# Seven-product down projection of a decoder trunk: other product signs, DMA-accumulated weight sums, a new buffer layout and a new last chunk

## Chip, cores and metric

The kernel runs on one NeuronCore of a Trainium2 chip. The metric is the device time of one execution in microseconds. Profiled times are counted from the start of the profiled span, which is a little shorter than the execution's own time.

## The reference, cut to what matters

One decoder layer over 512 tokens of width 2048 (float32): a token mixer of four head groups, a cross-attention, and an MLP with a squared ReLU, then a final RMS norm. The change lies in the MLP and the norm after it; the rest of the layer is untouched.

```python
hn = rmsnorm(h, norm_mlp_g[l])                                   # h: 512 x 2048
u = jnp.square(jax.nn.relu(jnp.einsum('bld,df->blf', hn, w_up[l])))   # 512 x 8192
h = h + jnp.einsum('blf,fd->bld', u, w_down[l])                  # w_down: 8192 x 2048
return rmsnorm(h, norm_final_g)
```

## The kernel before

Every float32 matrix is split into a high part in float32r (a ScalarE copy that rounds) and a low part (VectorE, the value minus the high part). A product is then three TensorE matmuls: high by high, high by low, low by high.

**Up phase.** Eight chunks q of 1024 hidden channels, in four pairs each. `up_pair` runs two `gemm`s of 16 k-tiles over the token activations (`ah{k}`, `al{k}`, 16 tiles each of 2 KB per partition, from the pool "acts"; weights stream through `wr`, `wh`, `wl` of the pool "weights"). It then squares the ReLU on ScalarE into `z`, forms four combinations of token and channel blocks of `z` on VectorE (L976 to L979), splits all seven operands (L146, L147) and lets the POOL queue write them to DRAM (`ud`, L984).

**Down phase.** The 2x2x2 block product (two token halves, two halves of the chunk's channels, two halves of the 2048 output columns) is made with seven products instead of eight. For each chunk, `down_chunk` loads four weight blocks b22, b11, b12, b21, each as two tiles of 1 MB (halves j), and calls `down_product(q, idx, ...)` seven times, idx being 6, 0, 4, 5, 2, 3, 1, in the last chunk 6, 0, 4, 5, 3, 2, 1. A product loads its left operand (`u_load`: two DMAs of 512 KB on SP's queue, three buffers), and for four quarters (j, a) forms the weight combination in place if there is one (L1059, VectorE), rounds it (L1061, ScalarE) and takes the low part (L1062, VectorE) into one of five pairs of tiles `w2h`, `w2l` (`w_tiles`). Then come 48 matmuls into four PSUM banks (`two`, `sm` and `mm`, `acc` in turn), and `evict` adds the banks to accumulators x1 to x7 in SBUF (L1082, VectorE; in chunk 0 a plain ScalarE copy for those that start empty, L1080). The combinations cost 16 VectorE instructions in a chunk: 8 for idx 4 (b12 - b11, then b22 minus that), 4 for idx 5, 4 for idx 2.

Accumulators 2, 3, 4 and 7 start from the residual, which `h_block` transposes and stores to DRAM (`xd`) ahead of the up phase. `merge` (L1102) combines accumulators in the last three chunks. `tail_sums`, `tail_rs`, `tail_out` and `tail` make the final norm: sums of squares on ScalarE, the reciprocal root as a chain of small VectorE instructions, the scaling on VectorE, the store on SP's queue.

**Order and buffers.** A scheduler orders the instructions of each engine, before the kernel is built, by its own model of time; `urgent()` raises priority. At run time each engine and each DMA queue works through its list in order and waits for semaphores. The pools of the down phase lie over memory of the up phase: `down_a` (right side) over the residual tiles, free early in the up phase, and `down` (left side) over weights, activations and the tiles of `up_pair`; a tile waits for those that it covers. `hold` fixes which tiles lie at the bottom of `down`: accumulators 3, 1, 6, 7, then three of the five weight pairs, two of the three u buffers, and four of the eight raw tiles.

Of the kernel before, what the change touches and what calls it, by code (L numbers as in the profile page):

```python
# [20 lines left out]
P = 128  # L21
# [35 lines left out]
def trunk(ctx, tc, A, out):  # L57
# [7 lines left out]
    def pool(name, bufs=1, **kw):  # L65
        return ctx.enter_context(tc.tile_pool(name=name, bufs=bufs, **kw))
# [1 line left out]
    cp = pool("consts")  # L68
    wa = ExitStack()
    wp = wa.enter_context(tc.tile_pool(name="weights", bufs=1))  # L70
    ap = wa.enter_context(tc.tile_pool(name="acts", bufs=1))
    ps = pool("psum", space=PSUM)
    dr = pool("dram", space=DRAM)

# [255 lines left out]
    XL_ = [None] * KT  # L330

    def act_tiles(k):
        h = ap.tile([P, L], F32R, name=f"ah{k}")
        l = ap.tile([P, L], F32R, name=f"al{k}")
        return h, l

    rsx = cp.tile([P, L], F32, name="rsx")
# [402 lines left out]
    def attn_pair(c):  # L740
# [6 lines left out]
        for hd in range(2):  # L747
# [4 lines left out]
        k = ap.tile([P, L], F32, name=f"ah{8 + c % 2}")  # L752
        Q.dma_start(k, qkv_d[4 + c])
        q = []
        for hd in range(2):
            qz = ap.tile([P, L], F32, name=f"a{'hl'[hd]}{10 + c % 2}")
# [234 lines left out]

    zc.close()
    wa.close()
    p2 = pool("down", side="left", reuse_waits="tile")
    acc, first = {}, {}

    def slot(p, name, shape, dt):
        if name in first:
            return first.pop(name)
        return p.tile(shape, dt, name=name)  # L1000

    def hold(name, shape, dt):
        first[name] = p2.tile(shape, dt, name=name)

    ACC, RAW, UT, WT = [P, 2, 2, L], [P, 4, L], [P, 4, 256], [P, 2, L]
    for i in (3, 1, 6, 7):
        hold(f"x{i}", ACC, F32)
    for n in range(2, 5):
        hold(f"w2h{n}", WT, F32R)
        hold(f"w2l{n}", WT, F32R)  # L1010
    for n in range(1, 3):
        hold(f"u{n}0", UT, F32R)
        hold(f"u{n}1", UT, F32R)
    for n in range(4, 8):
        hold(f"wq{n}", RAW, F32)

    def acc_tile(i, eng=G):
        t = slot(p2, f"x{i}", ACC, F32)
        if (i, 0) in xd:
            for b in range(2):  # L1020
                eng.dma_start(t[:, b].rearrange("p j n -> p (j n)"), xd[i, b])
        acc[i] = t

    def flat(t):
        return t.rearrange("p a n -> p (a n)")

    raws, us, ws = [0], [0], [0]

    def raw2():
        n = raws[0] % 8  # L1030
        raws[0] += 1
        return slot(p2a if n < 4 else p2, f"wq{n}", RAW, F32)

    def u_load(q, idx):
        n = us[0] % 3
        us[0] += 1
        uu = []
        for i in range(2):
            t = slot(p2 if n else p2a, f"u{n}{i}", UT, F32R)
            Q.dma_start(t.bitcast(F32), ud[q, i][:, idx])  # L1040
            uu.append(t)
        return uu

    def w_tiles():
        n = ws[0] % 5
        ws[0] += 1
        return [slot(p2 if n > 1 else p2a, f"w2{c}{n}", WT, F32R) for c in "hl"]

    sets = [True]

    def down_product(q, idx, w, comb, acc_to, last=None):
        with urgent():
            uu = u_load(q, idx)
            wt = {}
            for j in range(2):
                for a in range(2):
                    r = [x[j][:, 2 * a:2 * a + 2] for x in (w,) + tuple(t for c in comb for t in c)]
                    for c in range(0, len(r) - 1, 3):
                        V.tensor_tensor(flat(r[c + 1]), flat(r[c + 2]), flat(r[c + 3]), op=OP.subtract)  # L1059
# [37 lines left out]
                    evict(j, b)  # L1097

    def merge(o, a, b, op):
        for h in range(2):  # L1100
            x, y, z = (flat(acc[i][:, h]) for i in (o, a, b))
            V.tensor_tensor(x, y, z, op=op)  # L1102

    def down_chunk(q):
        last = q == NC_ - 1
        with urgent():
            b22, b11, b12, b21 = [], [], [], []
            for b, i, k in ((b22, 1, 1), (b11, 0, 0), (b12, 0, 1), (b21, 1, 0)):
                for j in range(2):
                    t = raw2()  # L1110
                    Q.dma_start(t, A["w_down"][q, i, k, :, j])
                    b.append(t)
        if q == 0:
            acc_tile(3, Q)
            acc_tile(1)
            acc_tile(6)
        down_product(q, 6, b22, (), (-3,) if last else (3,))
        if q == 0:
            for i in (7, 4, 5, 2):
                acc_tile(i)  # L1120
# [4 lines left out]
        down_product(q, 4, b22, ((b12, b12, b11), (b22, b22, b12)), (6,))  # L1125
        down_product(q, 5, b11, ((b11, b22, b11),), (7,))
        if last:
            merge(3, 3, 6, OP.add)
            merge(7, 7, 6, OP.add)
            merge(4, 7, 4, OP.subtract)  # L1130
            down_product(q, 3, b12, (), (3, 7))
            tail_sums(1, 1, 7)
            tail_sums(0, 1, 3)
            down_product(q, 2, b22, ((b22, b22, b21),), (-4,))
            tail_sums(1, 0, 4)
            tail_rs(slice(2, 4))
            down_product(q, 1, b21, (), (2,), tail)
        else:
            down_product(q, 2, b22, ((b22, b22, b21),), (4,))
            down_product(q, 3, b12, (), (5,))  # L1140
            if q == NC_ - 2:
                merge(7, 7, 5, OP.add)
                merge(4, 4, 5, OP.add)
                merge(3, 5, 3, OP.subtract)
            down_product(q, 1, b21, (), (2,))

    ssq = cp.tile([P, 4, 4], F32, name="sx")
    rf = cp.tile([P, 4], F32, name="rf")
# [3 lines left out]

    def tail_sums(t, i, a):
        if not fin:
            fin["g"] = flat(raw2())
            Q.dma_start(fin["g"], A["fin_row"].to_broadcast([P, D]))
            fin["sq"] = flat(raw2())
# [17 lines left out]
    def tail(b):  # L1175
        with urgent():
# [97 lines left out]
```

## Time and profile before

| | us |
|---|---|
| time, median of 3 runs (2136.93 to 2142.98) | 2141.01 |
| the profiled execution's own time | 2139.84 |
| its span | 2138.1 |
| TensorE busy (98% of the span) | 2090.8 |
| VectorE busy (72%) | 1546.4 |
| ScalarE busy (42%) | 905.3 |
| GpSimd busy (4%) | 84.7 |

A busy time is the union of an engine's instruction spans. Matmuls overlap in the pipeline (one takes 0.39 us from start to end, the next starts after some 0.23 us), so the distance from start to start says more than the duration.

### The profile page before, as it was taken

What the parts mean: (1) busy time and instruction counts of PE and PEld (TensorE: products, weight loads), DVE (VectorE), ACT (ScalarE), POOL (GpSimd) and SP (SyncE); (2) the same over time, 40 slices, a digit from 0 to 9 for tenths busy, and PEclk for the clock granted to TensorE, in tenths of its full rate; (3) what the DMA queues carried; (4) which work ended last, traced back from release to release, by engine and by line L of the source; (5) the groups of instructions that cost most, each with busy time, mean ns of one, the idle gap of its engine ahead of it and who ended that gap; (6) DMA issues with size and microseconds to landing.
All of it is one profiled execution on the core that took longest, in us unless ns stands there. A gap on an engine that the chain in (4) does not pass through costs nothing.

```text
span 2138.1 us, 24909 instructions
## 1 busy us (share of the span) xinstructions
PE 2090.8 (98%) x9340; PEld 1701.7 (80%) x9340; DVE 1546.4 (72%) x2203; ACT 905.3 (42%) x1227; POOL 84.7 (4%) x140
## 2 busy tenths in 40 slices
PE   8999999999999999999999999999999999999996
PEld 6777778777988788888888888887788888888885
DVE  7999999996757573544444444444898898898898
ACT  7565552557435453433332333323343333333333
POOL 0000000100000000100000010101000000000000
PEclk9999999999999999999999999999999999999998
DMA  8553325533433136855556565555846546546633
GB/s 306 170 174 116 113 87 167 178 109 99 146 101 118 33 118 217 288 191 173 193 167 198 167 196 167 188 181 189 309 175 248 186 175 238 216 138 243 230 118 119
DMA packets 106921, 371.30 MB, mean 174 GB/s; under 512 B 12576, under 2 KB 14240, under 8 KB 98480
## 3 DMA queue, kind: packets, MB, share of 16 engines
q1 hardware_dynamic: 88368, 300.49, 42.1%
q0 software_dynamic: 18432, 69.21, 9.1%
q8 instruction: 74, 1.21, 0.2%
q14 instruction: 47, 0.39, 0.1%
HBM read 293.09 MB, written 76.04 MB: 173 GB/s over the span
## 4 chain that ended last, share of the span: by engine, by line
PE 85%; DVE 7%; DMA 3%; ACT 2%; issue 1%; DVEq 0%; SPq 0%; ACTq 0%
PE mm L130 19%; PE mm L132 19%; PE mm L131 19%; PE mm L1072 3%; PE mm L1073 3%; PE mm L1071 3%; PE sm L1072 2%; PE two L1071 2%; PE two L1072 2%; PE two L1073 2%; PE sm L1073 2%; PE sm L1071 2%; DVE w2l L1062 2%; PE acc L481 1%; DVE x L1082 1%
## 5 line engine op out<-in xcount | busy, mean ns | idle before, releaser
L130 PE MATMUL mm<-ah,wh 128*128 128x512 f32 (+1 forms) x1920 | 743.0, 387 | 3.0 <-ACT cs L439 1.6
L132 PE MATMUL mm<-ah,wl 128*128 128x512 f32 (+1 forms) x1920 | 742.1, 387 | 3.7 <-DVE wl L126 3.7
L131 PE MATMUL mm<-al,wh 128*128 128x512 f32 (+1 forms) x1920 | 739.4, 385 | 0.0
L125 ACT ACTIVATE wh<-wr 128x1024 fp32r<-128x1024 f32 (+1 forms) x296 | 275.6, 932 | 578.2 <-PE mm L131 459.3
L126 DVE TENSOR_TENSOR wl<-wr,wh 128x1024 fp32r<-128x1024 f32 (+1 forms) x296 | 313.8, 1062 | 178.0 <-ACT wh L125 174.3
L132 PEld LDWEIGHTS mm<-ah,wl 128*128 128x128 f32 x1920 | 361.0, 188 | 79.8 <-DVE wl L126 6.4
L130 PEld LDWEIGHTS mm<-ah,wh 128*128 128x128 f32 x1920 | 361.0, 188 | 79.1 <-issue 4.1
L131 PEld LDWEIGHTS mm<-al,wh 128*128 128x128 f32 x1920 | 361.1, 188 | 73.5 <-issue 4.3
L1061 ACT ACTIVATE w2h<-wq 128x1024 fp32r<-128x1024 f32 x224 | 237.2, 1061 | 362.6 <-PE sm L1073 91.5
L1062 DVE TENSOR_TENSOR w2l<-wq,w2h 128x1024 fp32r<-128x1024 f32 x224 | 270.5, 1219 | 70.0 <-ACT w2h L1061 69.6
L973 DVE SCALAR_TENSOR_TENSOR r<-mm,rsx 128x512 f32<-128x512 f32 x64 | 44.2, 691 | 170.6 <-PE mm L132 169.8
L1059 DVE TENSOR_TENSOR wq<-wq,wq 128x1024 f32<-128x1024 f32 x128 | 153.4, 1217 | 3.0 <-DMA wq<-in_w_down 2.3
L1072 PE MATMUL mm<-w2l,u 128*128 128x512 f32 x336 | 132.1, 393 | 0.0
L1073 PE MATMUL mm<-w2h,u 128*128 128x512 f32 x336 | 131.8, 393 | 0.0
L1071 PE MATMUL mm<-w2h,u 128*128 128x512 f32 x336 | 130.2, 393 | 0.5 <-issue 0.5
L147 DVE TENSOR_TENSOR zl<-z,zh 128x1792 fp32r<-128x1792 f32 x32 | 64.8, 2026 | 55.7 <-ACT zh L146 51.3
L1071 PE MATMUL two<-w2h,u 128*128 128x512 f32 x224 | 87.6, 398 | 3.7 <-issue 3.7
L1072 PE MATMUL sm<-w2l,u 128*128 128x512 f32 x224 | 89.3, 399 | 1.0 <-DVE w2l L1062 1.0
L1071 PE MATMUL sm<-w2h,u 128*128 128x512 f32 x224 | 87.5, 399 | 2.1 <-ACT w2h L1061 2.1
L1072 PE MATMUL two<-w2l,u 128*128 128x512 f32 x224 | 89.0, 398 | 0.0
L1073 PE MATMUL two<-w2h,u 128*128 128x512 f32 x224 | 89.0, 398 | 0.0
L1073 PE MATMUL sm<-w2h,u 128*128 128x512 f32 x224 | 89.0, 397 | 0.0
(360 smaller groups left out, 2388.7 us busy)
## 6 DMA issues: line engine op xcount, KB each, us to landing
wr<-in_w_up SPq DMA_DIRECT2D x128, 512.0 KB, 3.8
wq<-in_w_down SPq DMA_DIRECT2D x64, 1024.0 KB, 6.5
u<-ud SPq DMA_DIRECT2D x112, 512.0 KB, 4.4
wr<-in_w_in SPq DMA_DIRECT2D x56, 512.0 KB, 4.2
ud<-zh POOLq DMA_DIRECT2D x32, 896.0 KB, 4.7
ud<-zl POOLq DMA_DIRECT2D x32, 896.0 KB, 8.2
wr<-in_w_out SPq DMA_DIRECT2D x64, 256.0 KB, 3.0
h<-in_xT SPq DMA_DIRECT2D x16, 256.0 KB, 6.0
```

What stands on the lines that cost most here:

```text
L125: S.activation(h, r, AF.Copy)
L126: V.tensor_tensor(l, r, h.bitcast(F32), op=OP.subtract)
L130: T.matmul(o, wh, xh, start=start, stop=False)
L131: T.matmul(o, wh, xl, start=False, stop=False)
L132: T.matmul(o, wl, xh, start=False, stop=stop)
L147: V.tensor_tensor(l, src, h.bitcast(F32), op=OP.subtract)
L1059: V.tensor_tensor(flat(r[c + 1]), flat(r[c + 2]), flat(r[c + 3]), op=OP.subtract)
L1061: S.activation(flat(h), flat(r[0]), AF.Copy)
L1062: V.tensor_tensor(flat(l), flat(r[0]), flat(h).bitcast(F32), op=OP.subtract)
L1071: T.matmul(o[2 * j + b], uh, h[:, p], start=a == 0 and p == 0, stop=False)
L1072: T.matmul(o[2 * j + b], uh, l[:, p], start=False, stop=False)
L1073: T.matmul(o[2 * j + b], ul, h[:, p], start=False, stop=a == 1 and p == 1)
```

## The change

The signs of the products are chosen anew, so that two of the weight combinations are sums of blocks as they lie in DRAM: b12 + b11 and (after idx 4 and 5 have used b22) b22 + b21. These two are made by DMAs from the POOL queue that add into the tile (`accum_op=OP.add`), two DMAs of 1 MB each; b11 and b21 are still loaded on their own as well. VectorE keeps 4 additions for idx 4 and 4 subtractions for idx 5. The order of a chunk is 6, 0, 4, 5, 3, 2, 1 throughout. The four raw pairs get fixed numbers that rotate by chunk: the tiles of b11 in one chunk hold b22 in the next, those of b12 hold b11, those of b22 hold b12; b21 keeps its own.

The activations of the up phase lie in two pools by k (0 to 7 and 8 to 15), and the down phase's left side becomes three pools: `down_w` over "weights", `down_x` over the first activations, `down` over the rest. All loads of accumulators go to SP's queue. In the last chunk, the scaling by the final gain of accumulator 3 and the output of token half 1 come ahead of the last product, and ScalarE does part of the last scaling.

```diff
-    ap = wa.enter_context(tc.tile_pool(name="acts", bufs=1))
+    aps = [wa.enter_context(tc.tile_pool(name=f"acts{i}", bufs=1)) for i in range(2)]
...
-            S.activation(x3, h_block(b, 1, j), AF.Copy, scale=-1.0)
-            S.activation(x7, h_block(b + 2, 1, j), AF.Copy)
-            V.tensor_tensor(x4, x7, h_block(b + 2, 0, j), op=OP.subtract)
+            S.activation(x3, h_block(b, 1, j), AF.Copy)
+            S.activation(x7, h_block(b + 2, 1, j), AF.Copy, scale=-1.0)
+            V.tensor_tensor(x4, h_block(b + 2, 0, j), x7, op=OP.subtract)
...
-            V.tensor_tensor(z[:, 3], z[:, 7], z[:, 2], op=OP.add)
+            V.tensor_tensor(z[:, 3], z[:, 7], z[:, 2], op=OP.subtract)
...
-            V.tensor_tensor(z[:, 6], z[:, 4], z[:, 1], op=OP.subtract)
+            V.tensor_tensor(z[:, 6], z[:, 4], z[:, 1], op=OP.add)
...
+    p2w = pool("down_w", side="left", reuse_waits="tile")
+    p2x = pool("down_x", side="left", reuse_waits="tile")
     p2 = pool("down", side="left", reuse_waits="tile")
...
+    home = {n: p2a for n in ("wq00", "wq01", "wq20", "wq21", "u00", "u01", "w2h0", "w2l0", "w2h1", "w2l1")}
+    home.update({n: p2x for n in ("wq10", "wq11", "u10", "u11", "w2h2", "w2l2")})
+    home.update({n: p2w for n in ("w2h3", "w2l3", "w2h4", "w2l4", "x3", "x1")})
...
-                    r = [x[j][:, 2 * a:2 * a + 2] for x in (w,) + tuple(t for c in comb for t in c)]
-                    for c in range(0, len(r) - 1, 3):
-                        V.tensor_tensor(flat(r[c + 1]), flat(r[c + 2]), flat(r[c + 3]), op=OP.subtract)
+                    r = [x[j][:, 2 * a:2 * a + 2] for x in (w,) + comb[1:]]
+                    if comb:
+                        V.tensor_tensor(flat(r[1]), flat(r[2]), flat(r[3]), op=comb[0])
...
     def down_chunk(q):
         last = q == NC_ - 1
+        b22, b11, b12, b21 = (raw2(n) for n in ((0, 1, 2, 3), (1, 2, 0, 3), (2, 0, 1, 3))[q % 3])
+
+        def load(b, i, k, eng=Q, **kw):
+            with urgent():
                 for j in range(2):
+                    eng.dma_start(b[j], A["w_down"][q, i, k, :, j], **kw)
+
+        load(b22, 1, 1)
+        load(b12, 0, 1)
+        load(b12, 0, 0, G, accum_op=OP.add)
+        load(b11, 0, 0)
+        if not q:
+            acc_tile(3)
+        down_product(q, 6, b22, (), (3,))
+        if not q:
             acc_tile(1)
             acc_tile(6)
+        load(b21, 1, 0)
         if q == NC_ - 3:
             merge(2, 2, 1, OP.add)
             merge(6, 6, 1, OP.add)
         down_product(q, 0, b11, (), (2, 6) if q >= NC_ - 3 else (1,))
...
+        down_product(q, 4, b22, (OP.add, b22, b22, b12), (6,))
         if last:
+            merge(3, 3, 6, OP.subtract)
+            merge(7, 7, 6, OP.subtract)
+            merge(4, 4, 6, OP.add)
+        down_product(q, 5, b11, (OP.subtract, b11, b22, b11), (-7, 4) if last else (7,))
+        load(b22, 1, 0, G, accum_op=OP.add)
+        down_product(q, 3, b12, (), (3, 7) if last else (5,))
+        if last:
             tail_sums(1, 1, 7)
             tail_sums(0, 1, 3)
+            with urgent():
+                for b in range(2):
+                    x = flat(acc[3][:, b])
+                    V.tensor_tensor(x, x, fin["g"][:, 1024:], op=OP.mult)
+        if q == NC_ - 2:
+            merge(4, 4, 7, OP.add)
+            merge(7, 5, 7, OP.subtract)
+            merge(3, 3, 5, OP.add)
+        down_product(q, 2, b22, (), (4,))
+        if last:
             tail_sums(1, 0, 4)
             tail_rs(slice(2, 4))
+            with urgent():
+                for b in range(2):
+                    tail_out(1, b, 1, 7)
+                    tail_out(1, b, 0, 4)
+        down_product(q, 1, b21, (), (2,), tail if last else None)
...
     def tail(b):
...
             tail_rs(slice(b, b + 1))
             tail_out(0, b, 0, 2)
-            tail_out(0, b, 1, 3)
-        tail_out(1, b, 1, 7)
-        tail_out(1, b, 0, 4)
+            x = flat(acc[3][:, b])
+            S.activation(x, x, AF.Copy, scale=rf[:, b:b + 1])
+            Q.dma_start(out[P * b:P * b + P, 1024:], x)
```

## Rows read from the trace of the kernel before

**Rows 1.** Page: busy time by engine, share of the span, instructions.
```profile
PE 2090.8 (98%) x9340; PEld 1701.7 (80%) x9340; DVE 1546.4 (72%) x2203; ACT 905.3 (42%) x1227; POOL 84.7 (4%) x140
```

**Rows 2.** Windows: an up stretch, chunks 0, 1, 2, 7, end; busy by engine, clock, DMA.
```profile
1080.00:1400.00 320.00, 320.00 (x1414) 265.05 (x1413) 141.63 (x161) 101.75 (x103) 25.89 (x29) 1.00 0.56 183
...
1485.80:1576.45 90.65, 83.78 (x338) 66.68 (x336) 73.76 (x72) 40.11 (x44) 5.00 (x8) 0.92 0.78 294
...
1653.96:1731.49 77.53, 77.53 (x337) 63.12 (x336) 67.77 (x73) 29.74 (x28) 0.00 (x0) 1.00 0.56 203
...
2041.60:2120.30 78.70, 78.15 (x338) 62.91 (x336) 74.59 (x95) 33.53 (x40) 0.00 (x0) 1.00 0.24 81
2120.30:2138.10 17.80, 0.00 (x0) 0.00 (x0) 13.37 (x34) 1.45 (x4) 0.00 (x0) 0.63 0.59 236
```

**Rows 3.** Timeline, TensorE, phase change: start, duration, instruction, idle time and releaser.
```profile
1485.80 0.40 PE L1071 MATMUL two<-w2h,u 128*128 128x512 f32 x1
...
1493.54 1.22 PE L1071 MATMUL sm<-w2h,u 128*128 128x512 f32 x2 [2.09 <-ACT w2h L1061]
1495.80 0.79 PE L1072 MATMUL sm<-w2l,u 128*128 128x512 f32 x1 [1.04 <-DVE w2l L1062]
...
1503.11 0.40 PE L1071 MATMUL mm<-w2h,u 128*128 128x512 f32 x1
...
1518.14 0.76 PE L1071 MATMUL two<-w2h,u 128*128 128x512 f32 x1 [3.74 <-issue]
...
1532.13 0.39 PE L1071 MATMUL mm<-w2h,u 128*128 128x512 f32 x1
```

**Rows 4.** Timeline, ScalarE and VectorE, phase change.
```profile
1488.77 1.06 ACT L1061 ACTIVATE w2h<-wq 128x1024 fp32r<-128x1024 f32 x1 [1.41 <-PE two L1073]
1489.74 1.69 ACT L146 ACTIVATE zh<-z 128x1792 fp32r<-128x1792 f32 x1
...
1491.45 2.02 DVE L147 TENSOR_TENSOR zl<-z,zh 128x1792 fp32r<-128x1792 f32 x1 [0.36 <-ACT zh L146]
1493.40 4.62 DVE L1062 TENSOR_TENSOR w2l<-wq,w2h 128x1024 fp32r<-128x1024 f32 x4
1497.94 8.03 DVE L1059 TENSOR_TENSOR wq<-wq,wq 128x1024 f32<-128x1024 f32 x7
...
1517.36 0.68 DVE L1082 TENSOR_TENSOR x<-x,two 128x512 f32<-128x512 f32 x1
```

**Rows 5.** Groups by line, VectorE, chunk 2: busy, mean ns, idle before.
```profile
L1062 DVE TENSOR_TENSOR w2l<-wq,w2h 128x1024 fp32r<-128x1024 f32 x28 | 33.9, 1221 | 9.7 <-ACT w2h L1061 9.7
L1059 DVE TENSOR_TENSOR wq<-wq,wq 128x1024 f32<-128x1024 f32 x16 | 19.2, 1218 | 0.0
```

**Rows 6.** DMA, chunks 2 and 3: share of 16 engines; issues, KB, us to landing.
```profile
q1 hardware_dynamic: 6336, 31.46, 56.3%
...
wq<-in_w_down SPq DMA_DIRECT2D x16, 1024.0 KB, 6.4
```

**Rows 7.** POOL's DMA issues beside a busy VectorE, timeline and DMA view.
```profile
1494.84 2.31 POOL L1021 DMA_DIRECT2D x<-xd  x4
...
x<-xd SPq DMA_DIRECT2D x2, 512.0 KB, 21.1
```

**Rows 8.** Timeline, TensorE's last matmul, then VectorE to the end.
```profile
2119.88 0.39 PE L1073 MATMUL acc<-w2h,u 128*128 128x512 f32 x1
...
2122.57 3.67 DVE L1170 SCALAR_TENSOR_TENSOR x<-x,rf,wq 128x1024 f32<-128x1024 f32 x3
2126.16 0.68 DVE L1082 TENSOR_TENSOR x<-x,acc 128x512 f32<-128x512 f32 x1
...
2127.47 0.19 ACT L1178 ACTIVATION_READ_ACCUMULATOR wq<-x 128x1 f32 x1
2129.34 0.15 DVE L1165 TENSOR_REDUCE ss<-sx 128x1 f32<-128x4 f32 x1
...
2131.65 2.48 DVE L1170 SCALAR_TENSOR_TENSOR x<-x,rf,wq 128x1024 f32<-128x1024 f32 x2
```

More of the change, by code (lines that the diff above doesn't have):

```diff
@@ L332, in act_tiles @@
     def act_tiles(k):
-        h = ap.tile([P, L], F32R, name=f"ah{k}")
-        l = ap.tile([P, L], F32R, name=f"al{k}")
+        h = aps[k // 8].tile([P, L], F32R, name=f"ah{k}")
+        l = aps[k // 8].tile([P, L], F32R, name=f"al{k}")
         return h, l
@@ L751, in attn_pair @@
             v.append(vz)
-        k = ap.tile([P, L], F32, name=f"ah{8 + c % 2}")
+        k = aps[1].tile([P, L], F32, name=f"ah{8 + c % 2}")
         Q.dma_start(k, qkv_d[4 + c])
@@ L755, in attn_pair @@
         for hd in range(2):
-            qz = ap.tile([P, L], F32, name=f"a{'hl'[hd]}{10 + c % 2}")
+            qz = aps[1].tile([P, L], F32, name=f"a{'hl'[hd]}{10 + c % 2}")
             G.memset(qz[64 - 64 * hd:128 - 64 * hd], 0.0)
@@ L993, in trunk, with slot, acc_tile @@
     wa.close()
+    p2w = pool("down_w", side="left", reuse_waits="tile")
+    p2x = pool("down_x", side="left", reuse_waits="tile")
     p2 = pool("down", side="left", reuse_waits="tile")
[L995 to L1018, printed above, removed]
+    acc = {}
+    home = {n: p2a for n in ("wq00", "wq01", "wq20", "wq21", "u00", "u01", "w2h0", "w2l0", "w2h1", "w2l1")}
+    home.update({n: p2x for n in ("wq10", "wq11", "u10", "u11", "w2h2", "w2l2")})
+    home.update({n: p2w for n in ("w2h3", "w2l3", "w2h4", "w2l4", "x3", "x1")})
+    def slot(name, shape, dt):
+        return home.get(name, p2).tile(shape, dt, name=name)
+    def acc_tile(i):
+        t = slot(f"x{i}", [P, 2, 2, L], F32)
         if (i, 0) in xd:
             for b in range(2):
-                eng.dma_start(t[:, b].rearrange("p j n -> p (j n)"), xd[i, b])
+                Q.dma_start(t[:, b].rearrange("p j n -> p (j n)"), xd[i, b])
         acc[i] = t
@@ L1025, in flat, with raw2 @@
         return t.rearrange("p a n -> p (a n)")
[L1027 to L1032, printed above, removed]
+    us, ws = [0], [0]
+    def raw2(n):
+        return [slot(f"wq{n}{j}", [P, 4, L], F32) for j in range(2)]
     def u_load(q, idx):
@@ L1038, in u_load @@
         for i in range(2):
-            t = slot(p2 if n else p2a, f"u{n}{i}", UT, F32R)
+            t = slot(f"u{n}{i}", [P, 4, 256], F32R)
             Q.dma_start(t.bitcast(F32), ud[q, i][:, idx])
@@ L1046, in w_tiles @@
         ws[0] += 1
-        return [slot(p2 if n > 1 else p2a, f"w2{c}{n}", WT, F32R) for c in "hl"]
+        return [slot(f"w2{c}{n}", [P, 2, L], F32R) for c in "hl"]
     sets = [True]
@@ L1099, in merge @@
     def merge(o, a, b, op):
-        for h in range(2):
-            x, y, z = (flat(acc[i][:, h]) for i in (o, a, b))
-            V.tensor_tensor(x, y, z, op=op)
+        with urgent():
+            for h in range(2):
+                x, y, z = (flat(acc[i][:, h]) for i in (o, a, b))
+                V.tensor_tensor(x, y, z, op=op)
     def down_chunk(q):
         last = q == NC_ - 1
-        with urgent():
-            b22, b11, b12, b21 = [], [], [], []
-            for b, i, k in ((b22, 1, 1), (b11, 0, 0), (b12, 0, 1), (b21, 1, 0)):
+        b22, b11, b12, b21 = (raw2(n) for n in ((0, 1, 2, 3), (1, 2, 0, 3), (2, 0, 1, 3))[q % 3])
+        def load(b, i, k, eng=Q, **kw):
+            with urgent():
                 for j in range(2):
[L1110 to L1114, printed above, removed]
+                    eng.dma_start(b[j], A["w_down"][q, i, k, :, j], **kw)
[7 more added lines that the diff above has]
+        if not q:
             acc_tile(1)
             acc_tile(6)
[L1117 to L1120, printed above, removed]
+        load(b21, 1, 0)
         if q == NC_ - 3:
@@ L1124, in down_chunk @@
         down_product(q, 0, b11, (), (2, 6) if q >= NC_ - 3 else (1,))
-        down_product(q, 4, b22, ((b12, b12, b11), (b22, b22, b12)), (6,))
-        down_product(q, 5, b11, ((b11, b22, b11),), (7,))
+        if not q:
+            for i in (7, 5, 4, 2):
+                acc_tile(i)
+        down_product(q, 4, b22, (OP.add, b22, b22, b12), (6,))
         if last:
[L1128 to L1131, printed above, removed]
+            merge(3, 3, 6, OP.subtract)
[5 more added lines that the diff above has]
+        if last:
             tail_sums(1, 1, 7)
             tail_sums(0, 1, 3)
-            down_product(q, 2, b22, ((b22, b22, b21),), (-4,))
+            with urgent():
[8 more added lines that the diff above has]
+        if last:
             tail_sums(1, 0, 4)
             tail_rs(slice(2, 4))
[L1137 to L1145, printed above, removed]
+            with urgent():
+                for b in range(2):
+                    tail_out(1, b, 1, 7)
+                    tail_out(1, b, 0, 4)
+        down_product(q, 1, b21, (), (2,), tail if last else None)
     ssq = cp.tile([P, 4, 4], F32, name="sx")
@@ L1154, in tail_sums @@
         if not fin:
-            fin["g"] = flat(raw2())
+            g, sq = raw2(NC_ % 3)
+            fin["g"], fin["sq"] = flat(g), flat(sq)
             Q.dma_start(fin["g"], A["fin_row"].to_broadcast([P, D]))
-            fin["sq"] = flat(raw2())
         with urgent():
```

## The prediction, made before the changed kernel ran

> **What bounds the kernel.** I read the page first, for the engine that fills the span: TensorE, 98% busy, VectorE next with 72% [rows 1]. Removing VectorE work therefore pays only where TensorE waits for it. Next I read windows, cut at the chunk borders of the down phase, for where TensorE does not run at its own pace [rows 2]. An up stretch makes 1414 matmuls in 320 us, 0.226 us each. Chunk 2 makes its 336 in 77.5 us, 0.231 each, with TensorE busy throughout and the clock at its higher level (1.00, 2.4 GHz); of the six chunks 1 to 6, all between 77.4 and 77.6 us, one stands in the rows. VectorE is at 67.8 of 77.5 us there, close to full but not the bound; its only idle time, 9.7 us, is spent waiting for ScalarE's roundings [rows 5]. Three stretches are worse: chunk 0 takes 90.65 us, 13.1 more than chunk 2; the last chunk 78.7 us, 1.2 more; and behind the last matmul stand 17.8 us without any. These 32 us are all that the change can win by waits; the other 2106 us are TensorE at its pace, and the matmuls are neither fewer nor shorter afterwards.
>
> **How the 13.1 us of chunk 0 arise.** I read TensorE's timeline across the phase change [rows 3]. The first product starts at 1485.80, runs its first half and then waits 2.09 us for a rounding of ScalarE and 1.04 us for a low part of VectorE. The matmuls behind the gap take 0.79 instead of 0.40 us: the granted clock, 0.92 over the chunk [rows 2], is for some microseconds at its lower level (1.2 GHz). The product takes 17.3 us (1485.80 to 1503.11) where a steady one takes 77.53/7 = 11.1: 6.2 us lost. The third product waits 3.74 us at 1518.14, again with slow matmuls behind; 1503.11 to 1532.13 are 29.0 us for two products, 6.9 us lost. Together the 13.1 us.
>
> The other engines say why [rows 4]. Gap 1: only two weight pairs (w2 0 and 1) lie in memory that is free early; the third rounding is made at 1488.77 and the fourth behind `zh` of the last up pair. The low parts stand behind `zl`, 2.02 us at 1491.45. Gap 2: the third product needs the banks of the first, whose first eviction runs only at 1517.36. VectorE was full until then, with seven combinations in a row (8.03 us from 1497.94) ahead of it; and accumulator 3, loaded by SP's queue among the raw tiles, took 21.1 us to land [rows 7].
>
> **Part 1, the layout.** The four weight pairs of the first product now lie in early memory (0, 1), over activations of k below 8 (2), and over `wr`, `wh`, `wl` (3). The last up gemm reads k 0 to 7 in its first 24 matmuls, so pair 2 is free 24 x 0.226 = 5.4 us before 1485.80, or more; a tile of `wh` or `wl` is free at the end of a unit of 24 matmuls, at the latest with the last up matmul. ScalarE's queue shows a wait before the third rounding even then [rows 4], so it has time; one rounding and one low part take 1.06 + 1.22 us. Pair 2 is needed half a product, 5.5 us, after the start and pair 3 8.3 us after it. Gap 1 should go. If the queue still puts `zh` and `zl` first, pair 3 comes at about 1494.6 (`zl` ends at 1493.4, a low part takes 1.2) against a need at 1494.1, and half a microsecond is lost. b22, b12 and the first accumulate use memory that is free early; b11 loads 5.4 us before the phase change instead of at it.
>
> **Part 2, fewer combinations.** 8 of 16 instructions of L1059 leave each chunk: 8 x 1.218 = 9.7 us of VectorE [rows 5]. In the steady chunks that is worth nothing: TensorE hides it, at 67.8 as at 58.1 us of 77.5. In chunk 0 it takes some 5 us from ahead of the first eviction (4 of 8 combinations of idx 4 go), and accumulator 3 no longer queues behind b12 and b21. Gap 2 should go too. Of 13.1 us I take 12.2 as won, 0.9 left for short waits. Bounds: 0 (both gaps only move) and 13.1.
>
> **Part 3, the accumulating DMAs.** No row shows such a DMA. A plain load of 1 MB lands in 6.4 us (median), and the queue's share of 56.3% for 31.46 MB over two chunks (155 us) prices a megabyte at 0.563 x 155.1 / 31.46 = 2.78 us of all 16 engines [rows 6]. The eight plain loads of a chunk stay, four accumulates (4.19 MB) are added. At the plain price (lower bound; nothing less than moving the bytes) the engines go from 43.7 to 55.3 us of 77.5, at twice it (I take this: the tile has to be read as well, nothing else is known to be added) to 67.0. They are full at (77.5 - 43.7)/4.19 = 8.1 us per megabyte, 2.9 times the plain price: there the transfers become the bound. The upper bound I set at 4 times plain, 43.7 + 46.6 = 90.3 us, 12.8 us per chunk over TensorE's.
>
> Are they in time? b22 + b21 goes out when idx 5's combinations have read b22, at the latest when its product starts; ScalarE may round the first quarter for idx 2 when a weight pair is free, about one product (11 us) later, and TensorE needs it after two products, 22 us. One half at twice the plain time is 13 us (2 x 6.4). b12 is loaded when idx 2's low parts are done, about two products before the chunk's end; two more products pass before idx 4 reads the sum: some 44 us, less the load's 6.4 to 13 us and the accumulate's 13 to 26 us. Both fit. What is queued behind on POOL is only the next accumulate, as the accumulator loads have moved to SP. Steady chunks: 0 us, bounds 0 and 8 x 12.8 = 102 us.
>
> The Trainium skill, "Collectives: The Full Stack", § on SDMA + CCE, says that the add in the DMA engine is free of cycles of its own but needs two source reads, so such transfers go at half the copy rate. No run so far shows it; by it the engines would be 67.0 us busy in a chunk and nothing would change in the sum.
>
> The issue itself is POOL's. Beside a VectorE that is full with the low parts of 1493.40 to 1498.02 [rows 4], POOL issued four DMAs in 2.31 us [rows 7], so 0.6 us each is hidden. "SBUF — State Buffer", § Who interferes with whom, in the Trainium skill, warns that DMAs issued from GpSimd can be starved by VectorE; for two-input instructions as here it says descriptor generation is spared, and the trace agrees by those 2.31 us.
>
> **Part 4, the last chunk and the tail.** Timeline at the end [rows 8]: the last matmul ends at 2120.3, but VectorE runs four scalings of token half 1 (L1170, the last three 3.67 us) before the last eviction at 2126.16. Then square, root chain (2129.34 to 2131.6, 2.3 us), two scalings (2.48 us, the later for nothing but accumulator 3) and 4.0 us from 2134.1 to the end for the store. Afterwards the four scalings come ahead of the last product's evictions, and accumulator 3's is on ScalarE (some 1.06 us as a copy, beside VectorE's 1.28). The shortest chain is 0.3 + 0.68 + square 0.8 (0.63 + 0.19, as to 2127.47) + 2.3 + 1.28 + 4.0 = 9.4 us: 8.4 won. If VectorE takes everything strictly in program order, the four scalings start when the sums of idx 2 are squared and rooted: last bank of idx 2 at 2109.2, evicted 2110.6, squared 2113.1, root 2115.4, scalings to 2120.4; then per token block 1.3 + 0.8 + 2.3 + 1.25 = 5.65 us, twice: 2131.7, store to 2135.7; 2.4 won. I take between: 5.0.
>
> VectorE's load ahead of that: 9.7 us less combinations, four more evictions (2.7 us), two gain multiplications (2.4) and the four scalings (4.9) brought forward: 74.6 + 0.3 = 74.9 of 78.7 us [rows 2]. It falls no further behind than now. The previous chunk starts it with 9.7 us more room, so of the last chunk's 1.2 us I take 0.6.
>
> **Costing nothing.** The sign edits replace one instruction by one of the same kind and shape. Merges stay 16 instructions. Splitting the pools issues nothing. Accumulator loads on SP are DMAs of 0.35 us issue on a queue that mostly waits.
>
> **The sum.** 12.2 + 5.0 + 0.6 - 0 = 17.8 us less: 2139.84 - 17.8 = 2122.0. That is the profiled execution's own time, 1.2 us under the median of the three runs; I state 2122.
>
> **Rivals.**
> (a) *The accumulates bind* (ends slower). Above 8.1 us per megabyte every chunk waits for its sums; at 4 times plain 2122 + 102 = 2224. Also below that price, if the sum for idx 2 lands over 22 us after issue, each chunk gets a gap; by rows 3 one costs 6.2 to 6.9 us with its slow clock, so three chunks use up the gain, and eight give 2122 + 8 x 6.5 = 2174. For it: no row prices an accumulate. Against: the room of 2.9. Chance 0.18.
> (b) *The phase change only moves.* The queues were ordered by a model of time; ScalarE and VectorE may still put the last up pair first, or a raw load may take the place of accumulator 3's. With nothing won there: 2139.84 - 5.6 = 2134.2; if the tail too keeps its order (2.4 won, nothing else), 2137.4. Chance 0.13.
> (c) *Half of it*: one gap goes, or the tail gives only its lower bound: 2139.84 - 6.5 - 3 = 2130, about 2126 to 2134. Chance 0.09.
> (d) The forecast, 2117 (all upper bounds: 13.1 + 8.4 + 1.2) to 2127: 0.60.
>
> **Chances and range.** About 0.3% (6.4 us) is what a measurement of this kernel can tell from no change; against the median, faster is under 2134.6. (d), (c) and a small part of (b) lie there: 0.70. The rest of (b): 0.12. (a): 0.18. The range 2115 to 2147 holds (b), (c), (d) and leaves out (a). The forecast's own range is 2117 to 2127.
>
> **What would show it.** Gap 1: third and fourth L1061 before 1485 or at least before `zh`, no clock under 1.00 in chunk 0. Gap 2: the first eviction of x3 before 1508. Accumulates: landing under 13 us in the steady chunks, DMA share near 0.86, chunks still 77.5 us, VectorE near 58 us in each. Tail: the four scalings ahead of TensorE's end, 9 to 15 us behind the last matmul. Wrong it would be by gaps before idx 2 or idx 4 in every chunk, a clock that falls there, or a chunk 0 above 80 us.

## The result, and the profile after

The changed kernel takes 2159.15 us (median of 4 runs, 2154.79 to 2160.12), against 2140.82 for the kernel before (4 runs): the ratio is 1.0084, 95% interval 1.0064 to 1.0104. It is slower by 0.8%, where 2122 was predicted. The profiled execution's own time is 2154.79, its span 2152.4, 14.3 us longer than that of before. It is the fastest of the four, so the stages below account for 14.3 of the 18.3 us between the medians.

The page of the changed kernel, its busy times:

```profile
PE 2088.5 (97%) x9340; PEld 1699.7 (79%) x9340; DVE 1479.9 (69%) x2143; ACT 907.7 (42%) x1229; POOL 109.3 (5%) x166
```

VectorE does 66.5 us less than in [rows 1], as the change intends; TensorE has as many matmuls as before. Windows of the changed kernel: a stretch early in the up phase, chunks 0, 2 and 7, the end (columns as in [rows 2]):

```profile
860.00:892.00 32.00, 23.48 (x94) 18.49 (x93) 18.08 (x22) 10.90 (x11) 4.56 (x6) 0.84 0.90 281
1494.94:1594.10 99.16, 80.09 (x337) 64.14 (x336) 54.37 (x55) 38.34 (x42) 5.37 (x6) 0.91 0.83 276
1671.62:1749.15 77.53, 77.53 (x338) 63.12 (x336) 59.41 (x64) 29.73 (x28) 3.47 (x4) 1.00 0.80 263
2059.24:2136.94 77.70, 77.70 (x337) 62.92 (x335) 71.27 (x93) 34.10 (x42) 1.72 (x2) 1.00 0.40 121
2136.94:2152.40 15.46, 0.00 (x0) 0.00 (x0) 9.17 (x30) 3.04 (x5) 0.00 (x0) 0.62 0.68 271
```

The same early stretch in the kernel before:

```profile
860.00:892.00 32.00, 32.00 (x143) 26.51 (x142) 20.96 (x24) 13.97 (x15) 4.46 (x5) 1.00 0.90 317
```

Two places have lost time. Early in the up phase TensorE is 8.5 us idle in 32, at a clock of 0.84; before it was busy throughout. Chunk 0 takes 99.2 us in place of 90.65 [rows 2]. The steady chunks are as before, the last one is 1.0 us shorter, the stretch behind the last matmul 2.3 us.

To compare stages across executions I count the up stretch from the last transposition ahead of the up gemms to the first down product. By line, the last of the 64 transpositions, first in the changed kernel, then in the kernel before (duration ns, first and last start):

```profile
L946 PE MATMUL sm<-ident,h x64: 270/272/273, 798.4 to 842.5; 128*128 128x128 f32 x64
```

```profile
L946 PE MATMUL sm<-ident,h x64: 270/272/273, 800.3 to 844.4; 128*128 128x128 f32 x64
```

The first product starts at 1494.94 and before at 1485.80 [rows 3], so the up stretch is 652.4 us against 641.4: 11.0 lost. Then 8.5 lost in chunk 0, 1.0 and 2.3 won at the end; the part up to the last transposition, where the change alters only signs and the split of a pool, happened to be 1.9 shorter. 11.0 + 8.5 - 1.0 - 2.3 - 1.9 = 14.3.

**The early stall.** TensorE's timeline there (start, duration, idle time and releaser):

```profile
877.24 0.50 PE L130 MATMUL mm<-ah,wh 128*128 128x512 f32 x1 [2.39 <-ACT wh L125]
...
884.16 0.80 PE L132 MATMUL mm<-ah,wl 128*128 128x512 f32 x1 [6.13 <-DVE wl L126]
```

VectorE's and POOL's timelines give the chain behind the 6.13 us:

```profile
880.15 2.02 DVE L147 TENSOR_TENSOR zl<-z,zh 128x1792 fp32r<-128x1792 f32 x1 [4.57 <-DMA ud<-zl]
...
882.89 1.22 DVE L126 TENSOR_TENSOR wl<-wr,wh 128x1024 fp32r<-128x1024 f32 x1
```

```profile
857.97 2.05 POOL L1098 DMA_DIRECT2D wq<-in_w_down  x2
863.25 0.94 POOL L984 DMA_DIRECT2D ud<-zl  x1 [3.24 <-DVE zl L147]
```

The low part `wl` that TensorE wants stands on VectorE behind `zl`. `zl` waits for its buffer, whose contents the write issued at 863.25 is still taking away: it lands (its data are all in place) 16.8 us later, where the kernel before took 7.0. Ahead of it on POOL's queue stand the two accumulates for chunk 0's b12, issued at 857.97. POOL's queue is not all of it: the next two weight tiles `wr`, loaded on SP's queue, land after 11.4 and 12.0 us, in the kernel before after 5.8 and 4.7.

The 2.39 us are ScalarE's rounding of `wh`:

```profile
875.61 0.63 ACT L974 ACTIVATE z<-r 128x512 f32<-128x512 f32 x1 [6.04 <-DVE r L973]
876.15 1.04 ACT L125 ACTIVATE wh<-wr 128x1024 fp32r<-128x1024 f32 x1
```

The square ahead of it comes no later than before (33.1 us behind the last transposition in both kernels). But in the kernel before two roundings stand ahead of that square in ScalarE's list, here they stand behind it. The tile to be rounded landed only at 875.5, so here the order itself costs no more than 0.6 us; e4 below has the same order and the same 2.39 us although its tile landed 3.7 us ahead of the rounding.

**The phase change.** TensorE's timeline, chunk 0:

```profile
1494.94 0.40 PE L1057 MATMUL two<-w2h,u 128*128 128x512 f32 x1
...
1506.05 0.40 PE L1057 MATMUL mm<-w2h,u 128*128 128x512 f32 x1
...
1518.95 0.73 PE L1057 MATMUL mm<-w2h,u 128*128 128x512 f32 x2 [1.63 <-ACT w2h L1047]
1520.21 0.50 PE L1058 MATMUL mm<-w2l,u 128*128 128x512 f32 x1 [0.53 <-DVE w2l L1048]
...
1539.73 0.80 PE L1057 MATMUL two<-w2h,u 128*128 128x512 f32 x1 [16.91 <-DMA u<-ud]
```

SP's queue in the same stretch:

```profile
1506.01 11.94 SPq L1026 DMA_DIRECT2D u<-ud  x4
1518.00 2.56 SPq L1098 DMA_DIRECT2D wq<-in_w_down  x2
1520.92 0.89 SPq L1026 DMA_DIRECT2D u<-ud  x2
1521.86 16.89 SPq L1009 DMA_DIRECT2D x<-xd  x6
```

Gap 1 is gone: the first product takes 11.1 us. In place of gap 2 TensorE waits 16.91 us for the left operand u of the third product (idx 4). It is issued at 1520.92, behind the operands of idx 5 and 3 (idx 3's waits for a free buffer) and two raw tiles, and lands 18.8 us later. In the built kernel its two tiles, `u20` and `u21`, lie over `zh` and `zl` of the last up pair, in the pool `down`.

### The profile page after: what moved, and what is told of

Its sections match the earlier page's. It is cut to its first block, busy times and chain, and to the rows that moved or that the text cites. A ratio compares the mean times of both kernels' runs of the same rounds, so it can differ in the third digit from the quotient of the medians.

```text
span 2152.4 us, 24931 instructions
## 1 busy us (share of the span) xinstructions
PE 2088.5 (97%) x9340; PEld 1699.7 (79%) x9340; DVE 1479.9 (69%) x2143; ACT 907.7 (42%) x1229; POOL 109.3 (5%) x166
## 4 chain that ended last, share of the span: by engine, by line
PE 82%; DVE 7%; DMA 5%; issue 2%; ACT 2%; SPq 0%; POOL 0%; ACTq 0%; DVEq 0%; POOLq 0%
PE mm L130 17%; PE mm L132 17%; PE mm L131 16%; PE mm L1058 4%; PE mm L1059 4%; PE mm L1057 4%; PE two L1057 2%; PE two L1058 2%; PE sm L1058 2%; PE sm L1057 2%; PE two L1059 2%; PE sm L1059 2%; DVE wl L126 2%; PE acc L1058 1%; PE acc L1057 1%
## 5 line engine op out<-in xcount | busy, mean ns | idle before, releaser
L132 PEld LDWEIGHTS mm<-ah,wl 128*128 128x128 f32 x1920 | 361.5, 188 | 84.8 <-DVE wl L126 11.1
L1045 DVE TENSOR_TENSOR wq<-wq,wq 128x1024 f32<-128x1024 f32 x64 | 77.7, 1223 | 16.9 <-DMA wq<-in_w_down 16.7
## 6 DMA issues: line engine op xcount, KB each, us to landing
wq<-in_w_down POOLq DMA_DIRECT2D x32, 1024.0 KB, 12.2
```

What stands on the lines that cost most here:

```text
L132: T.matmul(o, wl, xh, start=False, stop=stop)
L1045: V.tensor_tensor(flat(r[1]), flat(r[2]), flat(r[3]), op=comb[0])
```

## The experiments

Theory T1: two separate stalls of place and order, one at each spot, while the accumulating transfers in the steady chunks cost nothing. Rival R1: the accumulating transfers are too dear, and crowd out whatever stands beside them. Every edit also lets the scheduler order the lists anew, so a run can differ from the changed kernel in more than the lines shown. The stages of all profiled executions (us; "rest" is from chunk 1's start to the end of the span):

| kernel | up stretch | chunk 0 | rest |
|---|---|---|---|
| before | 641.4 | 90.7 | 561.7 |
| changed | 652.4 | 99.2 | 558.3 |
| e1 | 652.4 | 77.7 | 559.1 |
| e2 | 641.5 | 105.6 | 558.7 |
| e3 | 641.7 | 98.0 | 558.7 |
| e4 | 649.1 | 93.4 | 558.3 |
| e5 | 641.5 | 86.3 | 558.6 |
| e6 | 641.7 | 77.6 | 559.6 |
| e7 | 641.4 | 81.9 | 559.6 |
| e8 | 652.3 | 77.6 | 628.9 |
| e9 | 641.4 | 77.6 | 560.5 |

The part ahead of the up stretch has the same work in all of them, but for signs, and took 842.5 to 852.1 us, so a single span says less than its stages; the medians and ratios (each to runs of the kernel before on the same chip) average over it.

**e1, the third product's left operand early.**

```diff
-    home.update({n: p2w for n in ("w2h3", "w2l3", "w2h4", "w2l4", "x3", "x1")})
+    home.update({n: p2w for n in ("w2h3", "w2l3", "w2h4", "w2l4", "x3", "u20", "u21")})
```

> The homes of tiles are exchanged: x1 lies in the general pool, the left operands u20 and u21 of the third product (idx 4) in the memory that is free at the start of the down phase, so that their loads stand on SP's queue ahead of idx 3's and idx 5's left operands. Nothing else changes; the early up phase keeps its 9 us. Theory T1 (two stalls of place and order: the third product's left operand lies over the last up pair's tiles and is issued behind a wait): the operand lands before 1515 us of the span, the wait of 16.9 us goes and most of the slow clock behind it, chunk 0 takes 79 to 85 us in place of 99.2, the time is 2139 to 2146 us against 2159 for the changed kernel. Rival R1 (the accumulating transfers themselves crowd the DMA engines, so something is late whatever the order): another tile of the phase change is late in its place, chunk 0 stays over 93 us, the time over 2152 us. A third outcome, x1 in the general pool waits in its turn: a gap before idx 2, chunk 0 at 85 to 95 us.

Measured: 2139.23 us (10 runs), ratio 0.9982 (0.9971 to 0.9993). The window of chunk 0 in e1:

```profile
1496.10:1573.75 77.65, 77.65 (x338) 63.12 (x336) 52.51 (x54) 37.17 (x41) 5.35 (x6) 1.00 0.92 325
```

Chunk 0 takes 77.65 us, better than T1's 79 to 85, and TensorE has no wait left in it, with all accumulates in place and the DMA engines at 0.92, busier than in the changed kernel (0.83). Exchanging the homes of u20, u21 and x1 wins the 21.5 us: the wait of 16.91, smaller waits of 1.63 and 0.53, and the slow clock behind them. R1 falls for this spot: nothing else came late instead. The early stall stays, 11.0 us.

**e2, chunk 0's sum on VectorE.** b12 + b11 of chunk 0 only; its two accumulates go.

```diff
-        load(b12, 0, 0, G, accum_op=OP.add)
+        if q:
+            load(b12, 0, 0, G, accum_op=OP.add)
...
+        if not q:
+            with urgent():
+                for j in range(2):
+                    for a in range(2):
+                        x, y = (flat(t[j][:, 2 * a:2 * a + 2]) for t in (b12, b11))
+                        V.tensor_tensor(x, x, y, op=OP.add)
```

> Chunk 0 alone forms b12 + b11 on VectorE (four additions more there); its accumulating transfers into b12 go. All other accumulates stay, and b22 and b12 are still loaded early in the up phase. T1: of the 9.1 us that the early up phase lost, the part that the two accumulates cause goes (4 to 9 us), if the plain early loads cause it, under 3 us goes. Chunk 0 keeps its wait for the third product's left operand (95 to 104 us). Time 2150 to 2156 us in the first case, 2156 to 2162 in the second. R1 (accumulates themselves cause both stalls): all 9 us of the early up phase go, and chunk 0 changes little, since its second accumulate stays.

Measured: 2156.65 us, ratio 1.0061 (1.0044 to 1.0078). The up stretch is 641.5 us: all of the 11.0 comes back, more than the 4 to 9 that T1 expected and as R1 had it. Chunk 0 keeps its wait (19.92 us for u) and takes 105.6 us, 6.4 more than in the changed kernel and above the 95 to 104 expected; so the time misses T1's 2150 to 2156 by 0.65.

**e3, the rotation exchanged.**

```diff
-        ... in ((0, 1, 2, 3), (1, 2, 0, 3), (2, 0, 1, 3))[q % 3])
+        ... in ((0, 2, 1, 3), (2, 1, 0, 3), (1, 0, 2, 3))[q % 3])
```

> The rotation of raw tiles is exchanged, so that chunk 0's b12 lies in the other early pool and b11 in the first: no load of b12 and no accumulate can go out in the early up phase, they move to the phase change. T1: the early up phase wins 5 to 9 us (first down product near 1487 to 1490 in place of 1494.9); the phase change keeps the third product's wait or gets a worse one, since two accumulates more stand there: chunk 0 at 99 to 115 us, time 2150 to 2165 us. R1: what the early phase wins, chunk 0 loses in full (transfer time is only moved): the time stays within 4 us of 2159.

Measured: 2149.03 us, ratio 1.0028 (1.0016 to 1.0040). The up stretch is 641.7 us, again all 11.0 back, although as many raw tiles are still loaded early (b11 in b12's stead). Chunk 0 does not pay for it: 98.0 us, 1 us under T1's 99 to 115, as the time is 1 us under T1's range; R1's 2155 to 2163 falls. In e2 and e3 POOL's early queue holds no accumulate, and no wait of TensorE is left there. Both also have their early roundings ahead of the square on ScalarE again, and idx 4's first combinations, which wait 2.88 us for an accumulate early in the changed kernel, out of the early part of VectorE's list; none of this was tried apart from the accumulates.

**e4, plain loads for accumulates.**

```diff
-        load(b12, 0, 0, G, accum_op=OP.add)
+        load(b12, 0, 0, G)
...
-        load(b22, 1, 0, G, accum_op=OP.add)
+        load(b22, 1, 0, G)
```

> All accumulating transfers become plain loads of the same bytes from the same place (the additions are left out, so the output is not the reference's). T1: both stalls stay for the most part, as their place and order stay: early up phase 6 to 9 us lost, chunk 0 at 93 to 99 us, time 2150 to 2159 us. R1: an accumulate costs about twice a plain load on the DMA engines; with plain loads both stalls fall to half or less: early up phase under 5 us, chunk 0 under 88 us, time under 2145 us. In the steady chunks both theories expect 77.5 us; the landing of these transfers falls from 12.2 us towards the 6 to 8 us of plain loads.

Measured: 2151.46 us, ratio 1.0037 (1.0023 to 1.0052). Early loss 7.7 us in place of 11.0, chunk 0 93.4 us, with 9.45 us of waiting for u in place of 16.91. All three lie in T1's ranges: the same bytes as plain loads, in the same place and turn, keep 7.7 of 11.0 us early and 15.9 of 21.7 us of chunk 0's excess over 77.5. The rest, 3.3 and 5.8 us, goes with the accumulate's dearer price. Early, the write of `zl` lands after 12.6 us in place of 16.8, and TensorE waits 1.88 us for `wl` in place of 6.13; the 2.39 us for `wh`, which are ScalarE's order, stay whole.

That price shows in the DMA view over chunks 1 to 6 (465.1 us each; queue: packets, MB, share of 16 engines; issues: KB, median us to landing). The changed kernel, where q0 holds only accumulates:

```profile
q0 software_dynamic: 3456, 25.17, 27.1%
...
wq<-in_w_down SPq DMA_DIRECT2D x48, 1024.0 KB, 8.0
u<-ud SPq DMA_DIRECT2D x85, 512.0 KB, 5.8
wq<-in_w_down POOLq DMA_DIRECT2D x24, 1024.0 KB, 12.2
```

e4, where it holds the same bytes as plain loads:

```profile
q0 software_dynamic: 3456, 25.17, 14.3%
...
wq<-in_w_down POOLq DMA_DIRECT2D x24, 1024.0 KB, 7.1
```

0.271 x 465.1 / 25.17 = 5.01 us per megabyte against 0.143 x 465.1 / 25.17 = 2.64: 1.9 times the plain price.

**e5, e1 and e2 together.**

> The moved left operands of e1 and chunk 0's sum b12 + b11 on VectorE of e2, together. T1 (two separate stalls, each with its own cause): both go, so the stretch from the last transposition ahead of the up gemms to the first down product takes 641.5 us (652.4 in e1), chunk 0 stays at 77.6 to 83 us (four additions of 1.22 us more on VectorE, 4.9 us, ahead of the third product), the time is 2126 to 2133 us. Rival (the early transfers only change places: what leaves the early up phase comes back at the phase change): chunk 0 at 86 us or more and the time within 3 us of e1's 2139.

Measured: 2137.51 us, ratio 0.9974 (0.9963 to 0.9985). The up stretch is as T1 had it, chunk 0 at 86.3 us and the time are not: both meet the rival's figures. TensorE waits 1.63 us for an eviction on ScalarE and 5.11 us for a low part there, and VectorE's timeline shows what stands ahead of the low part:

```profile
1544.45 0.69 DVE L1068 TENSOR_TENSOR x<-x,mm 128x512 f32<-128x512 f32 x1 [13.58 <-DMA x<-xd]
```

An accumulator's load: in the newly made order SP issues the operand of a later product, which waits for its buffer (1520.80), and raw tiles (1521.73) ahead of the accumulators' loads. These go out from 1523.47, 36.0 us behind the first product's start where e1 has 24.7, and land in 16.8 us (median). The rival's figures are met, but not by its cause: the two early accumulates are gone here and came back nowhere; another load was put too late on SP's queue.

**e6, e1 and e3 together.**

> The moved left operands of e1 and the exchanged rotation of e3, together: all accumulates stay, but the two of chunk 0 into b12 now go out at the phase change. T1: up stretch 641.5 us, chunk 0 at 77.6 to 84 us, the time 2126 to 2134 us. Rival (the accumulates' own traffic, 20.8 us of all engines for the four of a chunk, crowds the phase change as soon as it moves there): a gap before the third product or before idx 2 of 6 us or more with its slow clock, chunk 0 at 86 us or more, the time 2136 us or more.

Measured: 2130.64 us, ratio 0.9945 (0.9930 to 0.9960). Windows of chunks 0 and 1:

```profile
1490.45:1568.07 77.62, 77.62 (x337) 63.03 (x336) 56.17 (x57) 36.83 (x41) 5.97 (x7) 1.00 1.02 349
1568.07:1645.60 77.53, 76.87 (x333) 62.26 (x332) 60.18 (x65) 29.38 (x28) 3.44 (x4) 1.00 0.91 284
```

Both stalls are gone. Chunk 0 now carries four accumulates, the DMA engines are full in it, and TensorE does not wait once in it: the rival falls. In chunk 1 it waits once, 0.66 us for a left operand.

**e7, all sums on VectorE,** on e1's layout: no accumulate anywhere; `vsum(x, y)` adds the tiles of y to those of x in four VectorE instructions.

```diff
-        load(b12, 0, 0, G, accum_op=OP.add)
...
+        vsum(b12, b11)
         down_product(q, 4, b22, (OP.add, b22, b22, b12), (6,))
...
-        load(b22, 1, 0, G, accum_op=OP.add)
+        vsum(b22, b21)
```

> On e1's layout all accumulating transfers go and VectorE forms both sums in every chunk (16 combinations per chunk, as in the kernel before). T1: the steady chunks stay at 77.5 us with VectorE 68 us busy, so the accumulates had won nothing there; the up stretch is back at 641.5 us; b21 is now needed as a tile before idx 2 of chunk 0 and stands late in the queue, so chunk 0 may lose up to 8 us: 2126 to 2138 us. Rival R3 (taking 9.7 us from VectorE per chunk is what keeps TensorE fed in the new layout): gaps in steady chunks, each over 77.7 us, time over 2140 us.

Measured: 2132.14 us, ratio 0.9955 (0.9939 to 0.9972). Its chunk 2:

```profile
1646.56:1724.10 77.54, 77.54 (x338) 63.12 (x337) 67.70 (x73) 29.74 (x28) 0.00 (x0) 1.00 0.56 203
```

77.5 us with VectorE at 67.7: the accumulates win nothing in a steady chunk, and R3 falls. Chunk 0 loses 4.2 us (TensorE waits 1.63 us for an eviction on ScalarE, 1.39 and 0.38 us for low parts). On e1's layout, doing without the accumulates is the faster by some 6 us by the stages (11.0 won in the up stretch, 4.2 lost in chunk 0, 0.5 behind it), because it also ends the early stall. Against e6, which keeps them out of the early up phase, it makes no difference that these runs can tell (2132.14 and 2130.64, same chip).

**e8, accumulates twice,** in chunks 1 to 7 on e1's layout.

```diff
         load(b12, 0, 0, G, accum_op=OP.add)
+        if q:
+            load(b12, 0, 0, G, accum_op=OP.add)
...
         load(b22, 1, 0, G, accum_op=OP.add)
+        if q:
+            load(b22, 1, 0, G, accum_op=OP.add)
```

> On e1's layout every accumulating transfer of chunks 1 to 7 is issued twice (the sums are then not those of the reference; chunk 0 is unchanged). The engines' share of a steady chunk in the changed kernel is 54.4% plain and 25.8% accumulating (42.2 and 20.0 us of 77.5). T1 (the accumulate costs 1.9 times a plain byte and has room): with 40 us more than half full turns into 42.2 + 40.0 = 82.2 us, the transfers become the bound, a chunk takes 82 to 90 us and the time is 2175 to 2230 us. If an accumulate's price were mostly waiting and not engine time, the chunks would stay at 77.5 us and the time at 2139.

Measured: 2211.26 us (2 runs), ratio 1.0318 (1.0298 to 1.0339). One chunk's length of e8, from one wait of TensorE to the next, and the wait at its end:

```profile
1786.49:1871.36 84.87, 79.92 (x337) 64.58 (x337) 58.90 (x64) 29.48 (x28) 6.91 (x8) 0.96 0.95 285
```

```profile
1871.36 0.79 PE L1059 MATMUL mm<-w2h,u 128*128 128x512 f32 x1 [4.95 <-DMA u<-ud]
```

84.9 us, engines at 0.95, near idle only for some 5 us of it, and TensorE waits for a transfer: the transfers are the bound. So the accumulate's price is engine time, and one per sum leaves room.

**e9, half of the tail's scalings on ScalarE,** on e6.

```diff
-                for b in range(2):
-                    x = flat(acc[3][:, b])
-                    V.tensor_tensor(x, x, fin["g"][:, 1024:], op=OP.mult)
+                for a in (7, 3):
+                    for b in range(2):
+                        x = flat(acc[a][:, b])
+                        V.tensor_tensor(x, x, fin["g"][:, 1024:], op=OP.mult)
...
-                    tail_out(1, b, 1, 7)
+                    tail_act(1, b, 7)
...
+    def tail_act(t, b, a):
+        x = flat(acc[a][:, b])
+        S.activation(x, x, AF.Copy, scale=rf[:, 2 * t + b:2 * t + b + 1])
+        r0 = 256 * t + P * b
+        Q.dma_start(out[r0:r0 + P, 1024:], x)
```

> e6 with one change in the tail: accumulator 7 too is multiplied by the gain while the last product runs (two instructions of 1.22 us on VectorE, earlier), and ScalarE, which waits 4 us there, does its scaling, so that two of the four scalings of 1.25 us leave VectorE's queue ahead of the last eviction. T1 for the tail (VectorE's order binds: scalings of token half 1, then the last eviction, then the root chain): 2.0 to 3.0 us less behind the last matmul (13.3 us in place of 15.5 to 16), time 2127 to 2130 us against e6's 2130.6. Rival (the earlier gain multiplications only delay VectorE's evictions by the same amount, or the last store's 5.5 us to landing is what ends): under 0.7 us won.

Measured: 2129.50 us (5 runs), ratio 0.9930 (0.9917 to 0.9944), not told apart from e6. The last matmul ends at 2113.8 and the span 15.9 us later, as in e6 (15.8). VectorE's last eviction starts at 2113.81 in e9, with no scaling ahead, and its last scaling stands 7.1 us behind the last matmul in place of 8.3. The DMA view says where that went, the first line being the engines' share in tenths over 40 slices. The last 20 us of e9 (2110 to 2130):

```profile
DMA  0000000000000079999999999999999999900000
...
out<-x SPq DMA_DIRECT2D x8, 512.0 KB, 4.3
```

The same of e6 (2108 to 2128):

```profile
DMA  0000000007999999999500004999999999800000
```

In e9 the engines are full from the first store to the last: eight stores, 4.19 MB, in some 10.5 us. In e6 they pause for some 2.5 us between two bursts of four, but the first burst starts 0.7 us behind the last matmul, in e9 only 3.4 us behind it. The root of token half 1, which the first stores need, is ready 1.2 us behind the last matmul in e9 and 1.5 us ahead of it in e6: its last steps stand on VectorE behind an eviction that waits 2.35 us for TensorE. So the rival that named the stores is right as far as they fill the last 10.5 us. That VectorE's order no longer counts is not shown: what would start the stores earlier and let them run without a pause was not tried.

## Why the prediction was wrong, point by point

Two steps failed: the early accumulates, which the sum holds at nothing, and "Gap 2 should go too". The forecast was 17.8 us less; the profile shows 14.3 more. Of the 32.1 us between them 20.7 lie in chunk 0 (12.2 won expected, 8.5 lost), 11.0 in the early up phase, 2.7 in the tail; -0.4 in the last chunk and -1.9 in the part ahead of the up stretch complete the sum. That these 1.9 us came out shorter is luck.

**Part 1, layout: right for gap 1, and the step that failed stands in it.** "b22, b12 and the first accumulate use memory that is free early" was read as free of cost. The memory was free, the DMA engines were not: at 0.90 in that stretch already before, with the writes of `ud` on the same queue as the accumulates. With the two accumulates of 1 MB there the stretch is 11.0 us longer; e2, which drops them, and e3, which moves them, each win all of it back. How it divides was not separated: the write on POOL's queue behind them takes 9.8 us longer to land than before, the loads on SP's queue 6 to 7 us longer, and the order of ScalarE's list holds 2.39 us even with plain loads (e4). The prediction had read no row of the early up phase, and its sum has no term for it.

**Part 2, "Gap 2 should go too": the step that failed.** Its two named causes did go: fewer combinations, and accumulator 3 loaded earlier. But the new layout laid the third operand buffer over the tiles that are freed last, and SP's queue put it behind three others; e1, which exchanges that place, wins 21.5 us. Rival (b) came near the mechanism (another load takes the place) and priced it at "nothing won". This load was issued only 1.9 us before TensorE ran out of work (1520.92 against 1522.82) and took 18.8 us to land; TensorE waited 16.91 us and ran at the slow clock after it (0.80 us a matmul in place of 0.40). The bound of that term, 0, should have lain below zero. With the operand in its right place the term holds: e6's chunk 0 is 13.0 us shorter than before, against 12.2 forecast. The accumulators' loads on SP's queue, also held at nothing, cost TensorE a wait of 5.11 us in e5's order and none in e6's. From the up stretch on, e6 is some 15 us shorter than before, against 17.8 forecast.

**Part 3, accumulating DMAs: right.** Twice the plain price was taken, 1.9 measured; the engines' share in a steady chunk is 0.80 against 0.86 forecast, the landing 12.2 us against "under 13", the steady cost 0 (e7, and chunks 1 to 6 at 77.5 us each). The limit of 2.9 times the plain price is not contradicted: doubled, at some 3.8 times, the transfers bind (e8); nothing was run between. Rival (a) is out. The Trainium skill, "Collectives: The Full Stack", § The bandwidth ceiling, says of a ReduceScatter that the add in the DMA engine needs two source reads and so runs at half the rate of a copy; the trace agrees, 5.01 against 2.64 us per megabyte.

**POOL's issue: right in what it cost.** In the steady chunks an accumulate takes POOL 0.87 us to issue (3.47 us for 4), a plain load of e4 0.54, and TensorE waits for neither. VectorE's combinations waited for an accumulate six times in chunks 2 to 6, 9.7 us in all, and TensorE hid it. The Trainium skill, "SBUF — State Buffer", § Who interferes with whom, infers that descriptor generation is spared beside two-input VectorE instructions; these rows do not contradict it.

**Part 4: 1.0 for the last chunk (0.6 forecast), 2.3 for the tail (5.0 forecast, 2.4 the lower bound).** VectorE in the changed kernel, the last matmul ending at 2136.94:

```profile
2135.49 4.87 DVE L1170 SCALAR_TENSOR_TENSOR x<-x,rf,wq 128x1024 f32<-128x1024 f32 x4
2140.35 0.68 DVE L1068 TENSOR_TENSOR x<-x,acc 128x512 f32<-128x512 f32 x1
...
2145.27 1.28 DVE L1170 SCALAR_TENSOR_TENSOR x<-x,rf,wq 128x1024 f32<-128x1024 f32 x1
```

This is the strict program order of the lower bound: four scalings, then the last eviction. The upper bound was out of reach, though, by an estimate from the stores. It took 4.0 us for the last store from before [rows 8]; here 5.85 us pass from the last scaling's end (2146.55) to 2152.4, as four stores meet there. In e9 eight stores keep the engines full for 10.5 us, 1.3 us each, so four alone take some 5.2. The term was mis-sized in part because the stores were priced one by one; the order of VectorE's list, at its lower bound, is the other part.

## What to carry to other kernels

A transfer moved to "memory that is free early" must be priced on the engines and the queue of that time: read the DMA share and what stands behind it on the queue there, not only the address. When a layout is made anew, list every tile that the first products need, with its place and its turn on each queue; removing the named cause of a gap can bring up the next late load, and its price can be nearly a whole landing time (16.91 of 18.8 us here), not zero. Work taken from an engine that is hidden wins nothing; here the accumulates take VectorE from 67.8 to 59.4 us in chunk 2 and leave TensorE at 77.5 us. An edit that lets the lists be ordered anew changes more than itself: e5 lost 8.7 us in chunk 0 to a load that its own lines do not name.

## What was not expected of the hardware

A full set of DMA engines is no stall by itself: in e6 they show 1.02 over chunk 0 and TensorE never waits, while the changed kernel stalls there at 0.83. Issuing an accumulating DMA costs POOL more than a plain one, 0.87 against 0.54 us. And the stages ahead of the up stretch, the same work in each kernel but for signs, differ by up to 9.6 us between profiled executions (842.5 to 852.1), more than most effects sought here.
